# Two heads' weights-times-values matmuls issued one behind the other, each on its half of TensorE's columns

## The chip, the cores and the metric

The kernel runs on one core of a Trainium2 chip. The metric is device time in microseconds (us), the median of several runs. The profiler records one execution of its own. PE is TensorE's matmul stream, PEld its weight loads, DVE VectorE, ACT ScalarE, POOL GpSimd, SP the engine that issues most DMAs.

## What is computed

Two decoder layers over 512 positions of width 1024. Layer 0's mixer joins sliding-window attention (8 query heads, 2 key-value heads of 64 columns) and stick-breaking attention (8 heads of 64). Then follow cross-attention to a memory, a feed-forward part, and layer 1 with another mixer. The part of the reference that matters here, shortened:

```python
def sliding_window_attention(q, k, v, sinks):      # 4 blocks of 128 queries; keys: own block and the one before
    s = jnp.einsum('bnqhgd,bnkhd->bnhgqk', qb, kb) * (HEAD_DIM ** -0.5)
    ...
    p = p / (jnp.sum(p, axis=-1, keepdims=True) + jnp.exp(sink - m))
    o = jnp.einsum('bnhgqk,bnkhd->bnqhgd', p, vb)

def stick_breaking_attention(q, k, v):
    for n in range(S // SB_BLOCK):                  # 4 blocks of 128 queries; keys: all up to the block's end
        z = jnp.einsum('bqhd,bkhd->bhqk', q[:, t0:t1], k[:, :t1]) * (HEAD_DIM ** -0.5)
        ...
        a = jnp.where(causal, jnp.exp(jax.nn.log_sigmoid(z) + log_after), 0.0)
        outs.append(jnp.einsum('bhqk,bkhd->bqhd', a, v[:, :t1]))
```

## The kernel before

All activations are held feature-major (features on partitions, 512 positions along the row). A projection (`proj_fm`, `proj_tm`, lines 176 to 178) is three matmuls per 128-row chunk, since each operand is kept as a high and a low part. The tile framework's scheduler orders each engine's instructions from the program: whatever is ready goes first by priority, so projections of other parts are strewn between the steps of the attention heads. Each engine then runs its list strictly in that order.

Both kinds of heads work in pairs. A pair has one tile `ps_ov` of 128 partitions by 512 positions in PSUM: the first head (`a=0`) writes partitions 0 to 63, the second (`a=1`) 64 to 127. The values have 64 columns, so a weights-times-values matmul has 64 stationary columns and stands on half of the array's columns; the profile shows its form as `128*64`. These operands are plain float32 and each such matmul is run as two passes, each with a weight load of its own; the profile counts passes.

**Window heads**, `swa_pair(i)`, four pairs. Per head: scores (lines 705, 706), softmax, seven transposes (732, 734) into two `ps_tr` tiles, a copy by ACT to `swpT` (736), and seven matmuls over 128 positions (740, 741). `swpT` has one buffer.

**Stick-breaking heads**, `sb_pair(c, ...)`, four pairs. Per head and query block `n`: scores (783, 784) into `ps_at`, two sigmoids (ACT, 786 and 789), triangular masks (POOL), a running product (DVE, 796) and a product (DVE, 798) that leaves the weights in `be0` to `be3`. Then, per key block `kb`, transposes of the blocks `n >= kb` into `ps_tr` (803), a copy by ACT to `sbaT` (805), and one matmul over 512, 384, 256 or 128 positions (806). `ps_tr` and `sbaT` have two buffers each. After the pair, `split` (203 on ACT, 204 on DVE) makes the parts `oh`, `ol` that the output projection reads.

```python
o = ps("ov")
for a in range(2):
    ...
    for kb in range(NT):
        ...
        T.matmul(o[hr, kb * P:], lhsT=vb[h // 4][:, kb, 64 * (h % 4):64 * (h % 4) + 64],
                 rhs=aT[:, kb:].rearrange("p a b -> p (a b)"), start=kb == 0, stop=kb == NT - 1)
```

`mixer0` runs the four window pairs, then the value projections, the four stick-breaking pairs with their projections (`qk_proj`), the output projection of the window heads (`out_proj(0, ...)`), the keys and values of the memory (`mem_prep`, lines 326 to 331, and `mem_kv`), and the output projection of the stick-breaking heads.

Of the kernel before, what the change touches and what calls it, by code (L numbers as in the profile page):

```python
# [18 lines left out]
P = 128  # L19
D = 1024  # L20
KC = D // P
S = 512
NT = S // P
# [10 lines left out]
def trunk(ctx, tc, x, mem, positions, norm_mix, norm_cross, norm_mem, norm_ffn,  # L34
# [30 lines left out]

    def f32(ap):
        return ap.bitcast(FP32)
# [5 lines left out]
    # Token order of the layer 1 mixer: chunks 0 and 2 forwards, then chunks 1 and 3 backwards.  # L73
# [6 lines left out]
    # ------------------------------------------------------------------ constants  # L80
# [67 lines left out]
    # ------------------------------------------------------------------ building blocks  # L148
# [152 lines left out]
    # ------------------------------------------------------------------ memory keys and values  # L301
# [77 lines left out]
    # ------------------------------------------------------------------ cross attention  # L379
# [78 lines left out]
    # ------------------------------------------------------------------ conv feed-forward  # L458
# [44 lines left out]
    # ------------------------------------------------------------------ layer 0 mixer  # L503
    def mixer0():
        W = ab_w_in[0]
        # the tiles of the normalized input hold the memory's parts, keys and values afterwards
# [7 lines left out]
        def rotary():  # L514
            # rotary tables
# [47 lines left out]
        # token-major input blocks and the first weight tile arrive interleaved  # L563
# [28 lines left out]
        # queries as high and low parts stacked by partition halves, keys as both halves' high parts and low parts  # L592
# [10 lines left out]
        # band mask: valid iff i < j <= i + WINDOW  # L603
# [24 lines left out]
        def rope(src, dst, g, nh, tab):  # L628
            cg, sg = tab
            ts = slice(2 * g, 2 * g + 2)  # L630
            V.tensor_tensor(out=dst, in0=src, in1=cg[:, ts].unsqueeze(2).to_broadcast([P, 2, nh, 64]), op=ALU.mult)
            bt = tl(sp, [P, 2 * S], "swpT", 1)[:, :2 * nh * 64].rearrange("p (t h d) -> p t h d", t=2, d=64)
            for s_ in range(2):
                a, b = slice(32 * s_, 32 * s_ + 32), slice(32 * (1 - s_), 32 * (2 - s_))
                V.tensor_tensor(out=bt[:, :, :, a], in0=src[:, :, :, b],
                                in1=sg[:, ts, b].unsqueeze(2).to_broadcast([P, 2, nh, 32]), op=ALU.mult)
            G.tensor_tensor(out=dst, in0=dst, in1=bt, op=ALU.add)

        # inverse norms per token and head
# [50 lines left out]
        def swa_pair(i):  # L690
            o = ps("ov")
            kvs = slice(64 * (i // 2), 64 * (i // 2) + 64)
            for a in range(2):
                h = 2 * i + a
                hr = slice(64 * a, 64 * a + 64)
# [31 lines left out]
                pT = tl(sp, [P, 2 * S], "swpT", 1).rearrange("p (n a q) -> p n a q", n=NT, a=2)  # L727
# [10 lines left out]
                for n in range(NT):  # L738
                    if n:
                        T.matmul(o[hr, n * P:(n + 1) * P], lhsT=va[:, n - 1, kvs], rhs=pT[:, n - 1, 1], start=True, stop=False)  # L740
                    T.matmul(o[hr, n * P:(n + 1) * P], lhsT=va[:, n, kvs], rhs=pT[:, n, 0], start=n == 0, stop=True)  # L741
# [23 lines left out]
        def sb_pair(c, qb, kb_):  # L765
            o = ps("ov")
            for a in range(2):
                hr = slice(64 * a, 64 * a + 64)
                h = 2 * c + a
                # high and low parts of the queries stacked against the high part of the keys twice  # L770
# [7 lines left out]
                at = []  # L778
                for n in range(NT):
                    wdt = (n + 1) * P  # L780
                    z = ps("at")
                    nq = slice(n * P, wdt)
                    T.matmul(z[:, :wdt], lhsT=qs[:, nq], rhs=ks[:, :wdt], start=True, stop=False)
                    T.matmul(z[:, :wdt], lhsT=qs[hr, nq], rhs=kl[hr, :wdt], start=False, stop=True)  # L784
                    be = tl(bp, [P, wdt], f"be{n}", 2)
                    A.activation(out=be[:, :wdt], in_=z[:, :wdt], func=AF.Sigmoid)
                    sn_ = tl(bp, [P, S + 1], "sbs", 2)
                    G.memset(sn_[:, wdt:wdt + 1], 1.0)
                    A.activation(out=sn_[:, :wdt], in_=z[:, :wdt], func=AF.Sigmoid, scale=-1.0)
                    dgs = slice(n * P, wdt)  # L790
                    G.affine_select(out=sn_[:, dgs], in_=sn_[:, dgs], pattern=[[-1, P]], compare_op=ALU.is_gt,
                                    fill=1.0, base=0, channel_multiplier=1)
                    G.affine_select(out=be[:, dgs], in_=be[:, dgs], pattern=[[-1, P]], compare_op=ALU.is_gt,
                                    fill=0.0, base=0, channel_multiplier=1)
                    ex_ = tl(bp, [P, S], "sbe", 2)
                    V.tensor_tensor_scan(out=ex_[:, wdt - 1::-1], data0=sn_[:, wdt:0:-1], data1=sn_[:, wdt:0:-1],
                                         initial=1.0, op0=ALU.mult, op1=ALU.bypass)
                    V.tensor_tensor(out=be[:, :wdt], in0=be[:, :wdt], in1=ex_[:, :wdt], op=ALU.mult)
                    at.append(be)
                for kb in range(NT):  # L800
                    pt = ps("tr", NT, P)
                    for n in range(kb, NT):
                        T.transpose(out=pt[:, n], in_=at[n][:, kb * P:(kb + 1) * P], identity=ident)  # L803
                    aT = tl(bp, [P, NT, P], "sbaT", 2)
                    A.copy(out=aT[:, kb:], in_=pt[:, kb:])
                    T.matmul(o[hr, kb * P:], lhsT=vb[h // 4][:, kb, 64 * (h % 4):64 * (h % 4) + 64],  # L806
                             rhs=aT[:, kb:].rearrange("p a b -> p (a b)"), start=kb == 0, stop=kb == NT - 1)
# [26 lines left out]
        # output projection: window heads first, then the stick-breaking heads  # L834
# [13 lines left out]
    # ------------------------------------------------------------------ layer 1 mixer  # L848
    def mixer1():
# [21 lines left out]
        # Level masks. A level with blocks of h positions pairs neighbouring blocks; sources lie in the earlier one:  # L871
        # the even block of a forward chunk, the odd block of a backward chunk.
        masks = []
        mi = tl(resid, [P, S], "nsq", 2)[:, :P]
        for lv in range(7):
# [3 lines left out]
            for c in range(2):  # L879
                mf = mi[:, c * 64:(c + 1) * 64].rearrange("p (b h) -> p b h", h=h)  # L880
                # 2hb + ch <= s <= 2hb + ch + h - 1
# [19 lines left out]
        def head_core(hd, F, KS, q, vs, e0_, res):  # L901
# [11 lines left out]
            for lv in range(7):  # L913
# [7 lines left out]
                # one stationary tile holds the sources of a forward chunk and, between them, of a backward chunk  # L921
# [81 lines left out]
        def core(pr, args):  # L1003
# [4 lines left out]
            while live:  # L1008
                # the values are projected once both heads' levels are through
                if step == 8:  # L1010
                    vs.append(vproj(pr))
                live = [g for g in live if next(g, g) is not g]
                step += 1
# [45 lines left out]
    # ------------------------------------------------------------------ the two layers  # L1059
# [44 lines left out]
```

## Time and profile before

| | |
|---|---|
| median of 3 runs | 1640.3 us (1640.19 to 1640.34) |
| span of the profiled execution | 1638.4 us |
| PE busy | 1619.5 us, 99% of the span |
| PEld, DVE, ACT, POOL busy | 82%, 62%, 43%, 12% |
| chain that ended last | PE 97%, DVE 1%, DMA 1% |
| granted clock from 80 us on | 1.00 |

The span runs from the first to the last instruction; the 1.9 us between it and the median lie around it. The window heads' matmuls run from 96 to 154 us, the stick-breaking heads' from 184 to 280 us. A row of the timeline gives the start, then the length, of instructions that follow each other with the same line and shape (`x2`: two of them); since matmuls are pipelined, the distance from one start to the next is what a matmul costs the stream, and the length is longer.

### The profile page before, as it was taken

The numbers are of one execution on the slowest core, as the hardware profiler recorded it, in microseconds if no ns is written. First come the engines' busy times: TensorE is split into PE (matmuls) and PEld (weight loads), VectorE is DVE, ScalarE is ACT, GpSimd is POOL, SyncE is SP. The second block draws the span as 40 slices with busy tenths as digits, with TensorE's granted clock in tenths as the row PEclk, the third lists the DMA queues.
The fourth block names the chain that finished last, engine by engine and source line by source line (L and its number), as shares of the span: only waits on it lengthen the run. The fifth ranks groups of instructions, "written<-read, shape, count | busy, mean of one in ns | idle before, by whom it ended". The sixth has DMA issues, their size and how long they took to land.

```text
span 1638.4 us, 21081 instructions
## 1 busy us (share of the span) xinstructions
PE 1619.5 (99%) x8298; PEld 1342.6 (82%) x8298; DVE 1019.0 (62%) x1662; ACT 707.7 (43%) x1246; POOL 201.4 (12%) x307
## 2 busy tenths in 40 slices
PE   7999999999999999999999999999999999999998
PEld 7988677888788888888789898998888788888887
DVE  6764884756576376366776676645556763674563
ACT  5464774555343244133543344543544441342341
POOL 3300341201200000000522133101002000000000
PEclk9999999999999999999999999999999999999999
DMA  6211322411322322322422221443113223223222
GB/s 190 78 42 39 129 78 70 140 52 52 103 93 88 103 89 92 103 82 73 121 66 72 78 78 52 129 155 103 56 48 103 89 92 103 84 96 103 79 82 71
DMA packets 144479, 145.57 MB, mean 89 GB/s; under 512 B 2844, under 2 KB 143837, under 8 KB 144381
## 3 DMA queue, kind: packets, MB, share of 16 engines
q1 hardware_dynamic: 143882, 143.98, 27.5%
q8 instruction: 66, 1.08, 0.3%
q0 software_dynamic: 96, 0.07, 0.1%
q14 instruction: 32, 0.26, 0.1%
q10 hardware_dynamic: 403, 0.18, 0.0%
HBM read 142.12 MB, written 2.10 MB: 88 GB/s over the span
## 4 chain that ended last, share of the span: by engine, by line
PE 97%; DVE 1%; DMA 1%; ACT 0%; issue 0%; SPq 0%; DVEq 0%
PE ps_pj L178 28%; PE ps_pj L176 28%; PE ps_pj L177 28%; PE ps_at L926 1%; PE ps_ov L806 1%; PE ps_tr L803 1%; PE ps_at L784 1%; DMA sbqk<-in_x_dram 1%; PE ps_at L176 1%; PE ps_at L178 1%; PE ps_at L177 0%; PE ps_ov L741 0%; PE ps_ov L958 0%; PE ps_at L906 0%; PE ps_tr L442 0%; PE ps_ov L177 0%
## 5 line engine op out<-in xcount | busy, mean ns | idle before, releaser
L177 PE MATMUL ps_pj<-xl,whi 128*128 128x512 f32 x1088 | 432.2, 397 | 0.0
L178 PE MATMUL ps_pj<-xh,wlo 128*128 128x512 f32 x1024 | 409.2, 400 | 0.0
L176 PE MATMUL ps_pj<-xh,whi 128*128 128x512 f32 x1024 | 403.6, 395 | 2.0 <-DVE hF L977 1.3
L164 ACT CAST whi<-wraw 128x1024 fp32r<-128x1024 f32 (+2 forms) x276 | 263.9, 1004 | 303.9 <-PE ps_pj L177 251.9
L165 DVE TENSOR_TENSOR wlo<-wraw,whi 128x1024 fp32r<-128x1024 f32 (+2 forms) x276 | 318.2, 1188 | 47.3 <-ACT whi L164 46.4
L177 PEld LDWEIGHTS ps_pj<-xl,whi 128*128 128x128 f32 x1088 | 204.4, 188 | 50.1 <-issue 1.0
L176 PEld LDWEIGHTS ps_pj<-xh,whi 128*128 128x128 f32 x1024 | 192.4, 188 | 47.2 <-DVE hF L977 1.9
L178 PEld LDWEIGHTS ps_pj<-xh,wlo 128*128 128x128 f32 x1024 | 192.4, 188 | 44.3 <-issue 1.0
L275 DVE TENSOR_TENSOR xT<-ps_pj,xT 128x512 f32<-128x512 f32 x80 | 53.8, 687 | 153.2 <-PE ps_pj L178 153.0
L177 PE MATMUL ps_pj<-hid,whi 128*128 128x512 f32 x352 | 138.0, 397 | 0.0
L178 PE MATMUL ps_pj<-hid,wlo 128*128 128x512 f32 x352 | 137.8, 397 | 0.0
L176 PE MATMUL ps_pj<-hid,whi 128*128 128x512 f32 x352 | 137.3, 397 | 0.0
L178 PE MATMUL ps_pj<-whi,xl 128*128 128x256 f32 x416 | 120.7, 292 | 1.7 <-DVE xl L226 1.6
L236 POOL TENSOR_TENSOR nacc<-nacc,nsq 128x512 f32<-128x512 f32 x36 | 52.4, 1456 | 523.3 <-ACT nsq L235 520.4
L466 DVE TENSOR_TENSOR fu<-ps_pj,rb 128x512 f32<-128x512 f32 x88 | 60.5, 692 | 90.2 <-PE ps_pj L178 90.1
L177 PE MATMUL ps_pj<-ol,whi 128*128 128x512 f32 x256 | 101.8, 398 | 0.0
L178 PE MATMUL ps_pj<-oh,wlo 128*128 128x512 f32 x256 | 101.5, 398 | 0.0
L176 PE MATMUL ps_pj<-oh,whi 128*128 128x512 f32 x256 | 99.6, 402 | 0.4 <-ACT oh L203 0.4
L468 ACT ACTIVATE fa<-fu,ccol 128x512 f32<-128x512 f32 x88 | 71.3, 814 | 59.3 <-DVE fu L466 59.3
L176 PE MATMUL ps_pj<-whi,xh 128*128 128x256 f32 x288 | 83.4, 291 | 0.0
L177 PE MATMUL ps_pj<-wlo,xh 128*128 128x256 f32 x288 | 82.9, 290 | 0.0
L178 PEld LDWEIGHTS ps_pj<-whi,xl 128*128 128x128 f32 x416 | 79.4, 192 | 3.4 <-DVE xl L226 2.0
(353 smaller groups left out, 2615.6 us busy)
## 6 DMA issues: line engine op xcount, KB each, us to landing
wraw<-in_ffn_w_up_dram SPq DMA_DIRECT2D x44, 1024.0 KB, 5.1
wraw<-in_xa_w_kv_dram SPq DMA_DIRECT2D x16, 1024.0 KB, 5.6
wraw<-in_ffn_w_down_dram SPq DMA_DIRECT2D x16, 1024.0 KB, 5.1
wraw<-in_hgrn_w_in_dram SPq DMA_DIRECT2D x16, 1024.0 KB, 5.6
wraw<-in_ab_w_in_dram SPq DMA_DIRECT2D x8, 1024.0 KB, 5.3
wraw<-in_xa_w_q_dram SPq DMA_DIRECT2D x8, 1024.0 KB, 5.2
wraw<-in_xa_w_o_dram SPq DMA_DIRECT2D x8, 1024.0 KB, 5.3
wraw<-in_ffn_w_down_dram SPq DMA_DIRECT2D x8, 768.0 KB, 4.8
```

What stands on the lines that cost most here:

```text
L164: A.copy(out=hi[:, k, c], in_=raw[:, k, c])
L165: V.tensor_tensor(out=lo[:, k, c], in0=raw[:, k, c], in1=f32(hi[:, k, c]), op=ALU.subtract)
L176: T.matmul(o, lhsT=lh, rhs=rh, start=first, stop=False)
L177: T.matmul(o, lhsT=lh, rhs=rl, start=False, stop=False)
L178: T.matmul(o, lhsT=ll, rhs=rh, start=False, stop=last)
L236: (V if c == KC - 1 else G).tensor_tensor(out=self.acc, in0=self.acc, in1=sq, op=ALU.add)
L275: V.tensor_tensor(out=xT[m], in0=o, in1=xT[m], op=ALU.add)
L466: V.tensor_tensor(out=u, in0=o, in1=rb, op=ALU.mult)
L468: A.activation(out=a, in_=u, func=AF.Identity, scale=conv_col(l, 2, ch), bias=bias_col(l, ch))
L784: T.matmul(z[:, :wdt], lhsT=qs[hr, nq], rhs=kl[hr, :wdt], start=False, stop=True)
L803: T.transpose(out=pt[:, n], in_=at[n][:, kb * P:(kb + 1) * P], identity=ident)
L806: T.matmul(o[hr, kb * P:], lhsT=vb[h // 4][:, kb, 64 * (h % 4):64 * (h % 4) + 64], rhs=aT[:, kb:].rearrange("p a b -> p (a b)"), start=kb ...
```

## The change

In both pairs the transposes and copies of both heads are made first, and then the matmuls of the two heads alternate, the second head's ahead of the first's. The helper `behind` adds an order edge without a semaphore, so that the scheduler keeps the first head's matmul after the second's. In the window pairs `swpT` gets a second buffer; in the stick-breaking pairs `be0` and `be1` get a third, and the matmuls are put under `tc.high_priority()`. The numbers and shapes of instructions stay as they are on every engine; their order changes on PE, ACT, DVE and POOL, and not on SP. Lines after the edits move down by 6 to 27.

```diff
+    def behind(ins, other):
+
+        tc.add_manual_dep(ins.ins if hasattr(ins, "ins") else ins, (other.ins if hasattr(other, "ins") else other).name,
+                          mybir.DependencyInfo(mybir.DependencyClass.NoSync, mybir.DependencyReason.DATA),
+                          reason="side by side")
...
-            bt = tl(sp, [P, 2 * S], "swpT", 1)[:, :2 * nh * 64].rearrange("p (t h d) -> p t h d", t=2, d=64)
+            bt = tl(sp, [P, 2 * S], "swpT", 2)[:, :2 * nh * 64].rearrange("p (t h d) -> p t h d", t=2, d=64)
...
-                pT = tl(sp, [P, 2 * S], "swpT", 1).rearrange("p (n a q) -> p n a q", n=NT, a=2)
+                pT = tl(sp, [P, 2 * S], "swpT", 2).rearrange("p (n a q) -> p n a q", n=NT, a=2)
+                pTs.append(pT)
...
-                for n in range(NT):
-                    if n:
-                        T.matmul(o[hr, n * P:(n + 1) * P], lhsT=va[:, n - 1, kvs], rhs=pT[:, n - 1, 1], start=True, stop=False)
-                    T.matmul(o[hr, n * P:(n + 1) * P], lhsT=va[:, n, kvs], rhs=pT[:, n, 0], start=n == 0, stop=True)
+
+            for n in range(NT):
+                cs_ = slice(n * P, (n + 1) * P)
+                for back in ((1, 0) if n else (0,)):
+                    for a in (1, 0):
+                        mm = T.matmul(o[64 * a:64 * a + 64, cs_], lhsT=va[:, n - back, kvs], rhs=pTs[a][:, n - back, back],
+                                      start=n == 0 or back == 1, stop=back == 0)
+                        if a:
+                            first = mm
+                        else:
+                            behind(mm, first)
...
-                    be = tl(bp, [P, wdt], f"be{n}", 2)
+                    be = tl(bp, [P, wdt], f"be{n}", 3 if n < 2 else 2)
...
-                for kb in range(NT):
+
+            for kb in range(NT):
+                aTs = []
+                for a in range(2):
                     pt = ps("tr", NT, P)
                     for n in range(kb, NT):
-                        T.transpose(out=pt[:, n], in_=at[n][:, kb * P:(kb + 1) * P], identity=ident)
+                        T.transpose(out=pt[:, n], in_=ats[a][n][:, kb * P:(kb + 1) * P], identity=ident)
                     aT = tl(bp, [P, NT, P], "sbaT", 2)
                     A.copy(out=aT[:, kb:], in_=pt[:, kb:])
-                    T.matmul(o[hr, kb * P:], lhsT=vb[h // 4][:, kb, 64 * (h % 4):64 * (h % 4) + 64],
-                             rhs=aT[:, kb:].rearrange("p a b -> p (a b)"), start=kb == 0, stop=kb == NT - 1)
+                    aTs.append(aT)
+
+                with tc.high_priority():
+                    for a in (1, 0):
+                        h = 2 * c + a
+                        mm = T.matmul(o[64 * a:64 * a + 64, kb * P:], lhsT=vb[h // 4][:, kb, 64 * (h % 4):64 * (h % 4) + 64],
+                                      rhs=aTs[a][:, kb:].rearrange("p a b -> p (a b)"), start=kb == 0, stop=kb == NT - 1)
+                        if a:
+                            first = mm
+                        else:
+                            behind(mm, first)
```

On PE, the first window pair before: the seven matmuls of the first head (its weights are `swpT_845`) stand alone, and the transposes of a later head follow.

```order
L177 MATMUL ps_pj_1507<-xl7_229,whi_1474 128x512
L741 MATMUL ps_ov_812<-swpT_845,va_242 64x128
L740 MATMUL ps_ov_812<-swpT_845,va_242 64x128
L741 MATMUL ps_ov_812<-swpT_845,va_242 64x128
L740 MATMUL ps_ov_812<-swpT_845,va_242 64x128
L741 MATMUL ps_ov_812<-swpT_845,va_242 64x128
L740 MATMUL ps_ov_812<-swpT_845,va_242 64x128
L741 MATMUL ps_ov_812<-swpT_845,va_242 64x128
L732 MATMUL ps_tr_897<-ident_70,swp_864 128x128
```

The same pair on PE with the change; `swpT_889` is the second head's, and line 711 is 705 of before.

```order
L711 MATMUL ps_at_1029<-kTh_240,qT0_238 128x128
L750 MATMUL ps_ov_812<-swpT_889,va_242 64x128
L750 MATMUL ps_ov_812<-swpT_845,va_242 64x128
L750 MATMUL ps_ov_812<-swpT_889,va_242 64x128
L750 MATMUL ps_ov_812<-swpT_845,va_242 64x128
L750 MATMUL ps_ov_812<-swpT_889,va_242 64x128
```

The alternation goes on to 14 matmuls; instead of eight groups of seven there are four of 14. The stick-breaking matmuls stood in 24 groups of one or two of the same head, and stand in 16 groups of two, one of each head.

On PE, the end of the last stick-breaking pair before: the second head's first matmuls, with the transposes for its next key blocks between them, and then the first of 30 projection matmuls.

```order
L806 MATMUL ps_ov<-sbaT,vb 64x512
L803 MATMUL ps_tr<-ident,be_2431 128x128
L803 MATMUL ps_tr<-ident,be_2446 128x128
L806 MATMUL ps_ov<-sbaT,vb 64x384
L803 MATMUL ps_tr<-ident,be_2446 128x128
L176 MATMUL ps_pj<-whi,xl_2681 128x256
L177 MATMUL ps_pj<-wlo,xl_2681 128x256
```

The same end with the change; `be_2420` is the second head's block `n=3` and `be_2405` its `n=2`. Lines 821, 829 and 133 are 803, 806 and 127 of before.

```order
L821 MATMUL ps_tr<-ident,be_2420 128x128
L829 MATMUL ps_ov<-sbaT,vb 64x512 x2
L821 MATMUL ps_tr<-ident,be_2390 128x128
L821 MATMUL ps_tr<-ident,be_2405 128x128
L821 MATMUL ps_tr<-ident,be_2420 128x128
L821 MATMUL ps_tr<-ident,be_2337 128x128
L821 MATMUL ps_tr<-ident,be_2352 128x128
L829 MATMUL ps_ov<-sbaT,vb 64x384 x2
L821 MATMUL ps_tr<-ident,be_2405 128x128
L821 MATMUL ps_tr<-ident,be_2420 128x128
L821 MATMUL ps_tr<-ident,be_2352 128x128
L829 MATMUL ps_ov<-sbaT,vb 64x256 x2
```

Behind them stand one transpose, line 133, the two 128-wide matmuls, and three projection matmuls that read this pair's `oh`. No projection matmul is left between these steps. Ahead of the first row stand, from the last score matmul of this pair on (784 of before), four transposes, nine projection matmuls over 512 positions and one more transpose.

## Rows read from the trace of the kernel before

**Rows 1.** The page: busy time by engine, and the chain that ended last.

```profile
PE 1619.5 (99%) x8298; PEld 1342.6 (82%) x8298; DVE 1019.0 (62%) x1662; ACT 707.7 (43%) x1246; POOL 201.4 (12%) x307
PE 97%; DVE 1%; DMA 1%; ACT 0%; issue 0%; SPq 0%; DVEq 0%
```

**Rows 2.** Busy time of each engine in two stretches, with granted clock.

```profile
80.00:160.00 80.00, 80.00 (x461) 66.81 (x460) 45.06 (x153) 44.56 (x114) 0.13 (x2) 1.00 0.13 41
160.00:290.00 130.00, 128.42 (x733) 95.64 (x732) 90.23 (x151) 84.84 (x191) 37.23 (x99) 1.00 0.29 91
```

**Rows 3.** What PE waited for: total us, times, longest.

```profile
PE ps_pj L326 <- DVE xl L331: 1.6, 1, 1.6
```

**Rows 4.** Passes of these matmuls by line, with counts and forms.

```profile
L740 PE MATMUL ps_ov<-swpT,va x48: 272/273/273, 96.1 to 154.0; 128*64 128x128 f32 x48
L741 PE MATMUL ps_ov<-swpT,va x64: 272/273/323, 95.8 to 154.2; 128*64 128x128 f32 x64
L806 PE MATMUL ps_ov<-sbaT,vb x64: 272/458/643, 183.7 to 280.3; 128*64 128x512 f32 x16, 128*64 128x384 f32 x16, 128*64 128x256 f32 x16, 128*64 128x128 f32 x16
```

**Rows 5.** PE's timeline around one window head's group.

```profile
104.04 0.43 PE L741 MATMUL ps_ov<-swpT,va 128*64 128x128 f32 x2
104.31 0.38 PE L740 MATMUL ps_ov<-swpT,va 128*64 128x128 f32 x2
104.53 0.38 PE L741 MATMUL ps_ov<-swpT,va 128*64 128x128 f32 x2
...
105.71 0.33 PE L732 MATMUL ps_tr<-ident,swp 128*128 128x128 f32 x1
105.88 0.27 PE L734 MATMUL ps_tr<-ident,swp 128*128 128x128 f32 x1
105.99 0.27 PE L732 MATMUL ps_tr<-ident,swp 128*128 128x128 f32 x1
```

**Rows 6.** PE's timeline around two stick-breaking matmuls.

```profile
251.22 1.07 PE L806 MATMUL ps_ov<-sbaT,vb 128*64 128x512 f32 x2
252.23 0.44 PE L803 MATMUL ps_tr<-ident,be 128*128 128x128 f32 x2
252.59 0.86 PE L806 MATMUL ps_ov<-sbaT,vb 128*64 128x384 f32 x2
253.38 0.33 PE L803 MATMUL ps_tr<-ident,be 128*128 128x128 f32 x1
```

**Rows 7.** PE's timeline: full weight loads, one column of work each.

```profile
327.20 0.95 PE L411 MATMUL ps_tr<-ones,xsq 128*128 128x1 f32 x8
328.01 0.37 PE L177 MATMUL ps_at<-kl,yh 128*128 128x256 f32 x1
```

**Rows 8.** Timelines of PE, ACT and DVE: one block's way from scores to weights.

```profile
261.47 0.49 PE L784 MATMUL ps_at<-sbkl,sbqs 64*128 64x512 f32 x1
261.89 0.39 PE L177 MATMUL ps_pj<-wlo,xl 128*128 128x256 f32 x1
262.00 0.60 ACT L786 ACTIVATE be<-ps_at 128x512 f32<-128x512 f32 x1 [0.20 <-PE ps_at L784]
264.74 0.69 DVE L798 TENSOR_TENSOR be<-be,sbe 128x512 f32<-128x512 f32 x1
```

**Rows 9.** The copy to sbaT: its lengths (ns), and one behind its transposes.

```profile
L805 ACT COPY sbaT<-ps_tr x32: 267/432/593, 179.4 to 276.3; 128x512 f32<-128x512 f32 x8, 128x384 f32<-128x384 f32 x8, 128x256 f32<-128x256 f32 x8, 128x128 f32<-128x128 f32 x8
274.69 0.44 PE L803 MATMUL ps_tr<-ident,be 128*128 128x128 f32 x2
275.22 0.37 ACT L805 COPY sbaT<-ps_tr 128x256 f32<-128x256 f32 x1 [0.28 <-PE ps_tr L803]
```

**Rows 10.** The last pair's end: its last passes, what follows, the split's cast.

```profile
279.69 0.86 PE L806 MATMUL ps_ov<-sbaT,vb 128*64 128x256 f32 x4
280.49 0.33 PE L127 MATMUL ps_tr<-ident,crow 128*128 128x128 f32 x1
280.60 0.59 ACT L203 CAST oh<-ps_ov 128x512 fp32r<-128x512 f32 x1 [4.06 <-PE ps_ov L806]
```

More of the change, by code (lines that the diff above doesn't have):

```diff
@@ L692, in swa_pair @@
             kvs = slice(64 * (i // 2), 64 * (i // 2) + 64)
+            pTs = []
             for a in range(2):
                 h = 2 * i + a
-                hr = slice(64 * a, 64 * a + 64)
                 pr = tl(sp, [P, NT, 256], "swp", 2)
@@ L766, in sb_pair @@
             o = ps("ov")
+            ats = []
             for a in range(2):
                 hr = slice(64 * a, 64 * a + 64)
-                h = 2 * c + a
                 orow = slice(64 - 64 * a, 128 - 64 * a)
@@ L778, in sb_pair @@
                 at = []
+                ats.append(at)
                 for n in range(NT):
```

## The prediction

> **What bounds the kernel now.** I read the page first, for the engine that is always busy and the chain that ended last: PE is busy 99% of the span, and 97% of the chain is PE [rows 1]. Time that PE saves is therefore time saved, if nothing makes it wait instead. Next the stretches where the changed matmuls stand: from 80 to 160 us, the window heads, PE is never idle; from 160 to 290 us, the stick-breaking heads, it is idle 1.6 us, and the granted clock is 1.00, the 2.4 GHz level, in both [rows 2]. The view of waits puts those 1.6 us down to one wait, in front of the transposes of the memory, for DVE [rows 3]. Then I listed the passes of the lines that the change moves [rows 4], and read PE's timeline around their groups for what one costs [rows 5, 6]. The durations are those of one execution with a span of 1638.4 us; the median of the runs is 1640.3 us, 1.9 us more, and I carry a difference of the span over to it as it is.
>
> **What the matmuls cost.** The window heads have 48 + 64 = 112 passes over 128 positions, the stick-breaking heads 16 of each of four widths [rows 4]. Inside a window group two passes start 0.22 us after the two before them, so a pass is 0.109; the group of 14 takes 105.71 - 104.04 = 1.67 us, and 14 x 0.109 is 1.52, so 0.15 is a fixed cost of the group [rows 5]. With it, the group of two 512-wide passes, 1.01 us, leaves 0.43 for a pass, and that of two 384-wide ones, 0.79 us, leaves 0.32 [rows 6]; cost goes with width, 0.107 per 128 positions, so the 256-wide pass is 0.215 and the four widths together are 1.075. A pass on 64 of the array's 128 columns costs what a full transpose of the same width does (105.88 to 105.99, 0.11 [rows 5]): half of the columns do nothing.
>
> **Fewer groups.** Around a group PE also loses time outside it: the first full transpose behind it takes 0.17 in place of 0.11 [rows 5], and in front, from two transposes to the next group, 0.36 - 0.17 - 0.11 = 0.08 too much [rows 6]. So a group costs 0.15 + 0.06 + 0.08 = 0.29 us in changing from full matmuls to half ones and back. There are 8 + 24 = 32 groups now and 4 + 16 = 20 then: 12 x 0.29 = **3.5 us saved**, whatever the halves do beside each other.
>
> **Side by side.** No row of before has matmuls of both halves next to each other, so I bound this. Nothing is saved if the halves take turns; half of all passes (112 x 0.109 + 16 x 1.075 = 29.4 us) is saved if two heads cost what one does: 14.7 us. I take what follows from starts in program order, as the timelines show them, with the two passes of a matmul one behind the other in their own half: the second pass of one head's matmul then runs beside the first pass of the other's. A window group of 28 passes lasts 15 passes, so 4 x 13 x 0.109 = **5.7 us** saved. A stick-breaking pair of four passes lasts three, since there is nothing to chain on to: 16 pairs save one pass each, 4 x 1.075 = **4.3 us**.
>
> In the window groups two weight loads must fit into each 0.109 us. Eight loads of 128 columns with one column of work each take 328.01 - 327.20 = 0.81 us, 0.10 for one, or 0.115 if the first ran ahead of the group [rows 7]; I take 0.11. One of 64 columns lies between half of that and all of it. I take half, since the first pass of a group, which must wait for its own successor's load, loses no more than some 0.05 of the 0.15 above; the other end is the second rival.
>
> The Trainium skill (TensorE: Matmul & The Clock Gate, Part 3, "Measured speedup vs the span model") reports three column tiles at 2.38 times the speed of one. An estimate from it, two tiles at the same share of the ideal, is 1.59 times, so a window group of 28 x 0.109 = 3.05 us would take 1.92 where I count 1.64, and the 5.7 us would be 4.5. No run here shows it yet.
>
> **New waits.** On PE the order now ends the last stick-breaking pair with no projection between its steps; before, 30 stood there. So each step that ACT makes is bare. A transpose's record ends 0.16 us after the next instruction could start (0.27 long, 0.11 apart [rows 5]); the copy starts 0.09 behind it (274.69 + 0.44 = 275.13, then 275.22 [rows 9]), takes 0.59 for 512 positions to 0.27 for 128 [rows 9], about 0.1 less for each 128; and I allow 0.1 more until PE starts, as long as the way from PE to ACT. Part is spent anyway: 0.1 in entering the group, and the transposes of the next block that stand between (two, one, one). That leaves 0.16 + 0.09 + 0.59 + 0.1 - 0.1 = 0.84 for kb = 0; 0.48 in place of 0.59 and 0.22 off give 0.51 for kb = 1; then 0.38 and 0.11 off, 0.52; then 0.27 and 0.11 off, 0.41. Together 2.3 us.
>
> Ahead of them, the weights of the last block are late. From the start of its score matmul to the end of the product that makes them it is 264.74 + 0.69 - 261.47 = 3.96 us in before [rows 8], with nothing else in its way; with 0.1 until PE starts, 4.06. PE now has behind that matmul its own 0.42 [rows 8], five transposes (0.6) and nine projection matmuls of 512 positions (0.23 each, 2.1): 3.1 us. It stands 0.95 us; 1.6 if DVE, which has a weight split and three products of other blocks in front, is late by as much as that.
>
> Behind them, the first projection that reads this pair needs the cast of `ps_ov`: 0.11 from the last group's end and 0.59 long [rows 10], then 0.1 to PE: 0.8 us. Twelve projection matmuls hid this before. Sum of the tail: 2.3 + 0.95 + 0.8 = **4.0 us lost**, between 2 and 6.
>
> The memory's transposes now stand between the steps of the first pair with hardly a projection near, where DVE has the same running products to make. The wait there was 1.6 us [rows 3]; it can vanish or double, and as the bare stretch is longer I take **1.0 us more**. Elsewhere the order leaves 4 to 39 projection matmuls around each group, and I cost the copies there, the extra buffers and the reordered start at nothing; without that cover a group would lose 0.4 to 0.9 us, as in the tail. What DVE, ACT and POOL do is not less or more than before, and they are busy 62% at most.
>
> **Sum.** 3.5 + 5.7 + 4.3 - 4.0 - 1.0 = 8.5 us. Span 1629.9, median **1631.8 us**, 0.5% less. About 0.2%, 3.3 us, is what a measurement of this kernel can tell from no change. Its own range, with the tail from 2 to 6, the memory's wait from -1.6 to +2.6 and the overlap from 8 to 13 us, is 1627 to 1636. Chance 0.58.
>
> **Rivals.**
>
> *The halves take turns.* Passes of the second half start only when those of the first are through, for instance because their weights can't be loaded while the array streams. Then the 10 us are gone and 3.5 - 5.0 = -1.5 is left: 1641.8, no change that can be told. For it: nothing in this trace shows two halves at work. Against it: in a window group each pass has its own weight load and still starts 0.109 behind the last, so loads do run under streaming there. Chance 0.20. The Trainium skill (TensorE: Matmul & The Clock Gate, Part 3, "The mechanism") says that weight loads overlap with running matmuls only where the row group differs; two column halves have the same rows, and by that rule this rival holds. The window groups' spacing does not agree with it.
>
> *Weight loads bound the window groups.* If a 64-column load takes as long as the 0.11 us of a 128-column one, four passes need 0.44 and nothing is saved there, nor in the 128-wide pairs (4 x 0.109 = 0.44): 3.5 + 3.9 - 5.0 = 2.4 saved, 1637.9. Chance 0.12; within 0.2% in most of these.
>
> *Changing halves costs like changing to half matmuls.* There are 13 such changes in each window group and one in each pair, 4 x 13 + 16 = 68. At 0.15 us, what a group loses inside it [rows 5], that is 10.2 us on top of halves that take turns: 1652, slower. It decides from 0.03 us per change, since the 1.5 us lost there need 1.8 more. Against it: the 0.15 goes with a change between forms, and within a group of one form starts are even. Chance 0.10. The Trainium skill (TensorEngine Tiling, "Key Properties") has a drain for a change of the tiling mode and not for one of the tile; the 0.29 us around each group agrees with the first half, and no row of before shows the second.
>
> **How the numbers follow.** The forecast, 0.58, is faster throughout. Of the second rival, 0.05 is faster and 0.07 within 0.2%; of the first, 0.19 within and 0.01 slower; the third is slower. Faster 0.63, same 0.26, slower 0.11. The range goes from 1627, the forecast's lower end, to 1642.5, past the first two rivals, and leaves out the third and the forecast's far ends, some 0.15.
>
> **What would show it.** Right: PE's busy time down by some 12 to 14 us; window groups of 28 passes that last 1.6 to 1.9 us and stick-breaking pairs 3 passes long, with passes of the second head starting beside the other's; 20 groups; PE idle some 4 us between 250 and 290 us, put down to ACT's copies, one DVE product and the last cast. Wrong: groups as long as the sum of their passes, a gap at each change of halves, or idle time in front of the other pairs, where I count projections as cover.

## The result and the profile after

| | before | changed |
|---|---|---|
| median (4 runs each) | 1640.24 us (1638.2 to 1640.34) | 1627.5 us (1626.29 to 1628.51) |
| ratio | | 0.9929, interval 0.9915 to 0.9943 |
| span of the profiled execution | 1638.4 us | 1626.6 us |

By these medians the change is worth 12.7 us, and 9.3 us where both kernels were run again on another chip (1638.3 and 1629.04, after_again below); 8.5 had been forecast. The direction and the place were right, and the sum was short. (Beside the experiments, on other chips, the kernel before had medians of 1638.3 to 1638.7; the ratio of each kernel below is to the runs of before on its own chip.)

The page after, busy times and chain, beside [rows 1]:

```profile
PE 1604.9 (99%) x8298; PEld 1332.4 (82%) x8298; DVE 1017.4 (63%) x1662; ACT 706.7 (43%) x1246; POOL 200.9 (12%) x307
PE 97%; DVE 1%; ACT 1%; DMA 1%; issue 0%; SPq 0%; POOL 0%; DVEq 0%
```

PE has as many passes as before and is busy 14.6 us less. PE's timeline of one window pair, then the weight loads of the same group, beside [rows 5]:

```profile
99.22 1.75 PE L750 MATMUL ps_ov<-swpT,va 128*64 128x128 f32 x28
100.90 0.33 PE L739 MATMUL ps_tr<-ident,swp 128*128 128x128 f32 x1
101.07 0.27 PE L741 MATMUL ps_tr<-ident,swp 128*128 128x128 f32 x1
```
```profile
99.22 1.51 PEld L750 LDWEIGHTS ps_ov<-swpT,va 128*64 128x64 f32 x28 [0.20 <-ACT ses L723]
```

28 passes last 100.90 - 99.22 = 1.68 us, in each of the four groups, where the 14 of one head lasted 1.67. Their 28 weight loads fit into 1.51 us. Two stick-breaking groups of four passes, beside [rows 6]:

```profile
248.23 1.08 PE L829 MATMUL ps_ov<-sbaT,vb 128*64 128x512 f32 x4
249.24 0.55 PE L821 MATMUL ps_tr<-ident,be 128*128 128x128 f32 x3
...
253.53 0.87 PE L829 MATMUL ps_ov<-sbaT,vb 128*64 128x384 f32 x4
254.33 0.44 PE L821 MATMUL ps_tr<-ident,be 128*128 128x128 f32 x2
```

Four passes last 1.01 and 0.80 us, as two did (1.01 and 0.79). In the trace's records of the 512-wide group, two passes start 7 ns apart, and the other two some 0.48 us later, again 7 ns apart. The records do not name the heads. The two passes of one head alone start one behind the other and fill 1.01 us [rows 6], so I read these as first pass beside first pass, then second beside second.

The two stretches, beside [rows 2], and what PE waited for, beside [rows 3]:

```profile
80.00:160.00 80.00, 80.00 (x480) 65.29 (x479) 48.82 (x153) 48.26 (x126) 2.89 (x10) 1.00 0.17 54
160.00:290.00 130.00, 125.62 (x745) 96.73 (x744) 93.48 (x150) 84.88 (x188) 40.60 (x96) 0.96 0.30 93
```
```profile
PE ps_at L798 <- ACT sbs L804: 1.8, 1, 1.8
PE ps_tr L821 <- DVE be L813: 0.7, 1, 0.7
PE ps_pj L182 <- ACT oh L209: 0.7, 1, 0.7
PE ps_ov L829 <- ACT sbaT L823: 0.7, 1, 0.7
```

Where there was one wait there are four: three of 0.7 us at the end of the last pair, where waits were forecast, and one of 1.8 us in the stretch of the memory's transposes, now in front of a score matmul. The third number from the end of the second window is new too: the granted clock is 0.96 where it was 1.00. PE's timeline around the wait, and the windows behind it:

```profile
175.59 0.38 PE L799 MATMUL ps_at<-sbkl,sbqs 64*128 64x256 f32 x1
177.78 0.62 PE L798 MATMUL ps_at<-sbks,sbqs 128*128 128x384 f32 x1 [1.81 <-ACT sbs L804]
...
182.02 1.97 PE L829 MATMUL ps_ov<-sbaT,vb 128*64 128x512 f32 x4
183.93 0.90 PE L821 MATMUL ps_tr<-ident,be 128*128 128x128 f32 x3
```
```profile
176.00:180.00 4.00, 2.22 (x6) 1.36 (x7) 3.94 (x7) 3.95 (x9) 0.73 (x4) 0.73 0.00 0
180.00:184.00 4.00, 3.86 (x10) 0.97 (x9) 4.00 (x8) 2.75 (x7) 0.88 (x3) 0.50 0.57 170
184.00:188.00 4.00, 4.00 (x19) 4.00 (x20) 2.48 (x5) 2.32 (x5) 0.00 (x0) 0.50 1.04 333
188.00:260.00 72.00, 72.00 (x515) 60.17 (x514) 48.57 (x78) 48.45 (x113) 25.22 (x60) 1.00 0.26 83
```

From 177.9 us on the clock is at 0.50, the 1.2 GHz level, for 10.2 us; the first 512-wide group falls into it and lasts 183.93 - 182.02 = 1.91 us in place of 1.01. PE is busy nearly all of that time, so about half of it, 5.1 us, is lost. Why PE waits is seen in ACT's queue, which has no gap there:

```profile
175.78 0.47 ACT L336 ACTIVATE xl<-ps_pj,gcol 128x256 fp32r<-128x256 f32 x1
176.27 0.62 ACT L790 CAST sbks<-sbks 64x512 fp32r<-64x512 f32 x1
176.92 0.47 ACT L336 ACTIVATE xl<-ps_pj,gcol 128x256 fp32r<-128x256 f32 x1
177.29 0.27 ACT L801 ACTIVATE be<-ps_at 128x128 f32<-128x128 f32 x1
177.45 0.28 ACT L804 ACTIVATE sbs<-ps_at 128x128 f32<-128x128 f32 x1
```

The two sigmoids that free a score buffer stand behind the memory's copies (336) and a cast of keys (790). PE's order has no projection left there: the window heads' projections ran out at 172 us, and those of the memory need these copies.

### The profile page after: what moved, and what is told of

It reads as the page before. It is cut to its first block, busy times and chain, and to the rows that moved or that the text cites. A ratio compares the mean times of both kernels' runs of the same rounds, so it can differ in the third digit from the quotient of the medians.

```text
span 1626.6 us, 21049 instructions
## 1 busy us (share of the span) xinstructions
PE 1604.9 (99%) x8298; PEld 1332.4 (82%) x8298; DVE 1017.4 (63%) x1662; ACT 706.7 (43%) x1246; POOL 200.9 (12%) x307
## 4 chain that ended last, share of the span: by engine, by line
PE 97%; DVE 1%; ACT 1%; DMA 1%; issue 0%; SPq 0%; POOL 0%; DVEq 0%
PE ps_pj L182 28%; PE ps_pj L184 28%; PE ps_pj L183 28%; PE ps_at L953 1%; PE ps_ov L829 1%; PE ps_at L799 1%; DMA sbqk<-in_x_dram 1%; PE ps_tr L821 1%; PE ps_at L182 1%; PE ps_at L184 1%; PE ps_at L183 1%; PE ps_ov L985 0%; PE ps_at L933 0%; PE ps_tr L448 0%; PE ps_ov L750 0%; PE ps_ov L183 0%
## 5 line engine op out<-in xcount | busy, mean ns | idle before, releaser
L475 DVE SCALAR_TENSOR_TENSOR fa<-fu,ccol,fa 128x511 f32<-128x511 f32 x88 | 65.6, 748 | 25.8 <-ACT fa L474 25.8
```

The lines of the kernel that those rows point to most:

```text
L475: V.scalar_tensor_tensor(out=a[:, 1:], in0=u[:, :S - 1], scalar=conv_col(l, 1, ch), in1=a[:, 1:], op0=ALU.mult, op1=ALU.add)
```

## The experiments

Two medians tell little here, since time at the 1.2 GHz level comes and goes between executions: the two traces of the changed kernel (the second is after_again) have 10.2 and 6.8 us of it behind 177 us, and ten of the thirteen traces have 3.4 us of it near 23 us, ahead of the attention heads. So beside the ratio I read from each trace the time from the start of the first window score to the start of PE's last instruction ("stretch"), and for how long the granted clock was at 0.50 in it:

| kernel | median us | ratio to before (interval) | stretch us | at 0.50, us |
|---|---|---|---|---|
| before | 1640.24 | | 1562.1 | 0 |
| changed | 1627.5 | 0.9929 (0.9915 to 0.9943) | 1552.7 | 10.2 |
| after_again | 1629.04 | 0.9941 (0.9926 to 0.9956) | 1551.4 | 6.8 |
| swa_only | 1634.03 | 0.9966 (0.9953 to 0.9979) | 1559.0 | 6.8 |
| sb_only | 1635.97 | 0.9986 (0.9976 to 0.9995) | 1558.5 | 6.8 |
| swa_serial | 1633.31 | 0.9967 (0.9956 to 0.9979) | 1558.2 | 6.8 + 3.4 |
| tail_ring | 1625.84 | 0.9920 (0.9905 to 0.9935) | 1549.3 | 6.8 |
| mem_spread | 1625.18 | 0.9917 (0.9902 to 0.9932) | 1548.2 | 0 |
| spread_ring | 1622.16 | 0.9898 (0.9884 to 0.9913) | 1545.9 | 0 |
| before_spread | 1637.62 | 0.9994 (0.9984 to 1.0003) | 1561.5 | 0 |
| mem_mix | 1624.34 | 0.9913 (0.9898 to 0.9927) | 1548.2 | 0 |
| mix_ring | 1621.84 | 0.9901 (0.9884 to 0.9917) | 1546.0 | 0 |
| warm8 | 1627.22 | 0.9930 (0.9915 to 0.9944) | 1550.8 | 3.4 |

**One kind of heads at a time.** Each kernel takes one of the two pair functions from the kernel before.

Swa_only, with `sb_pair` as before:

```diff
-for kb in range(NT):
-    aTs = []
-    for a in range(2):
+    for kb in range(NT):               # inside "for a in range(2)"
...
-    for a in (1, 0):
-        mm = T.matmul(o[64 * a:64 * a + 64, kb * P:], ...)
+        T.matmul(o[hr, kb * P:], ...)
```

> Only the window heads are paired; the stick-breaking heads stay as in the kernel before. Theory (two halves cost what one does, as the trace after shows): four groups of 1.67 us and four changes of 0.14 us around them are gone, 4 x 1.81 = 7.2 us saved, since PE is never idle in that stretch and no tail is bared: about 1633.0 us beside a kernel before of 1640.2. Rival (the new order of the rest does most of it): less than 4 us saved, 1636 or more. The clock's drop behind 176 us should not be there.

Sb_only, with `swa_pair` as before:

```diff
-for n in range(NT):
-    for back in ((1, 0) if n else (0,)):
-        for a in (1, 0):
-            mm = T.matmul(o[64 * a:64 * a + 64, cs_], ...)
+    for n in range(NT):                # inside "for a in range(2)"
+        if n:
+            T.matmul(o[hr, n * P:(n + 1) * P], lhsT=va[:, n - 1, kvs], ...)
+        T.matmul(o[hr, n * P:(n + 1) * P], lhsT=va[:, n, kvs], ...)
```

> Only the stick-breaking heads are paired; the window heads stay as in the kernel before. Theory: 16 pairs at half the cost (4 x 2.8 / 2 = 5.6 to 8.6 us, by whether a pair's 512-wide passes overlap wholly) and 8 changes of 0.29 us, 10.9 us in all, less some 2.7 us of bare steps at the end of the last pair and some 3 to 5 us of idle time and lower clock behind 176 us: about 1635 us beside 1640.2. If the drop of the granted clock behind 176 us comes from the bare stretch in the first stick-breaking pair, it is here too; rival: if it is missing, the saving is 10 us or more, 1630 or less.

By the medians they save 4.7 and 2.7 us of a median of before of 1638.69, by the ratios 5.6 and 2.3. Each profiled execution has 6.8 us at the lower clock near 181 to 192 us. With half of that added back, the stretches save 3.1 + 3.4 = 6.5 and 3.6 + 3.4 = 7.0 us. The first is near the 7.2 that was expected without a drop; two of its five executions show a granted clock of 1.000 over the whole span, and they take 1630.8 and 1631.4 us, some 6 less than the 1636.8 to 1637.8 of the four of before at that clock. Sb_only had the drop in its expectation, with 1635 us as the number: 5.2 us less than before, of which the medians show about half and the stretch 3.6. So each kind of heads pays, and in each profiled execution the drop takes half of it back. That swa_only has the drop was not expected: its stick-breaking pairs are those of before. But in its timeline no projection stands from 172 to 188 us; in that of before there is none from 182 to 189.5.

**Neighbours in the queue.** Still four groups; within one, first the seven matmuls (14 passes; the text on record calls them 14 matmul instructions) of the second head, then those of the first.

```diff
-for n in range(NT):
-    for back in ((1, 0) if n else (0,)):
-        for a in (1, 0):
+for a in (1, 0):
+    for n in range(NT):
+        for back in ((1, 0) if n else (0,)):
```

> The changed kernel, with the 14 matmul instructions of one head of a window pair issued ahead of the 14 of the other instead of in turns, still four groups. Theory (it is the neighbouring of the two halves that pays): a window group takes 28 x 0.109 + 0.15 = 3.2 us in place of 1.68, so 4 x 1.5 = 6.1 us are given back, 1633.6 where the changed kernel has 1627.5. Rival (halves overlap wherever they stand in the queue, or it is the smaller number of groups that pays): within 1.5 us of the changed kernel.

PE's timeline of its first group:

```profile
100.17 2.89 PE L750 MATMUL ps_ov<-swpT,va 128*64 128x128 f32 x28
102.99 0.33 PE L739 MATMUL ps_tr<-ident,swp 128*128 128x128 f32 x1
```

2.82 us in place of 1.68, in all four groups: 4 x 1.14 = 4.6 us are given back, and the stretch, with as long at the lower clock as the changed kernel, is 5.5 us longer; the other 0.9 is idle time that PE has more of between 160 and 200 us (2.86 and 1.95). The theory holds for the window groups, and the rival falls; the stick-breaking pairs had no such run. That it is 2.82 and not the 3.2 of all passes in a row has a cause in the records: at the change of heads, the first passes of the half that comes second in the order start between the last ones of the other. Of its time at 0.50, 3.4 us stand behind the end of the last pair, from 281.7 us on; the changed kernel, with the same waits there, has none in either trace.

**The end of the last pair.** Its second and fourth key block take other buffers.

```diff
-pt = ps("tr", NT, P)
+pt = ps("at" if c == 3 and kb % 2 else "tr", NT, P)
...
-aT = tl(bp, [P, NT, P], "sbaT", 2)
+if c == 3 and kb % 2:
+    aT = tl(bp, [P, S], "sbe", 2).rearrange("p (a b) -> p a b", b=P)
+else:
+    aT = tl(bp, [P, NT, P], "sbaT", 2)
```

> The changed kernel, but the last stick-breaking pair puts its second and fourth key block's transposes into the score buffers and their copies into the scan buffers, which are idle by then, so that they need not wait for the block before. Forecast of the prediction (each copy is bared, 2.3 us in all): 1.0 to 1.5 us less than the changed kernel. Rival (only the first copy, the last block's weights and the last cast are bared, which this edit leaves): within 0.6 us of the changed kernel, the waits of 0.7 us for the weights, the first copy and the cast unchanged.

PE's timeline at the end of the last pair, the changed kernel first, then tail_ring:

```profile
264.73 0.40 PE L798 MATMUL ps_at<-sbks,sbqs 128*128 128x512 f32 x1
...
269.07 0.33 PE L821 MATMUL ps_tr<-ident,be 128*128 128x128 f32 x1 [0.72 <-DVE be L813]
270.07 1.08 PE L829 MATMUL ps_ov<-sbaT,vb 128*64 128x512 f32 x4 [0.68 <-ACT sbaT L823]
271.08 1.07 PE L821 MATMUL ps_tr<-ident,be 128*128 128x128 f32 x5
272.20 0.87 PE L829 MATMUL ps_ov<-sbaT,vb 128*64 128x384 f32 x4
273.00 0.85 PE L821 MATMUL ps_tr<-ident,be 128*128 128x128 f32 x3
273.89 0.65 PE L829 MATMUL ps_ov<-sbaT,vb 128*64 128x256 f32 x4
...
276.28 0.96 PE L182 MATMUL ps_pj<-oh,whi 128*128 128x512 f32 x3 [0.68 <-ACT oh L209]
```
```profile
264.77 0.40 PE L798 MATMUL ps_at<-sbks,sbqs 128*128 128x512 f32 x1
...
269.12 0.33 PE L821 MATMUL ps_tr<-ident,be 128*128 128x128 f32 x1 [0.19 <-DVE be L813]
269.29 0.27 PE L821 MATMUL ps_at<-ident,be 128*128 128x128 f32 x1
270.12 1.08 PE L832 MATMUL ps_ov<-sbaT,vb 128*64 128x512 f32 x4 [0.57 <-ACT sbaT L826]
271.13 0.44 PE L821 MATMUL ps_tr<-ident,be 128*128 128x128 f32 x2
271.50 0.87 PE L832 MATMUL ps_ov<-sbe,vb 128*64 128x384 f32 x4
272.30 0.33 PE L821 MATMUL ps_at<-ident,be 128*128 128x128 f32 x1
...
274.22 0.96 PE L182 MATMUL ps_pj<-oh,whi 128*128 128x512 f32 x3 [0.69 <-ACT oh L209]
```

From the last block's scores to the first projection that reads the pair it is 276.28 - 264.73 = 11.55 us in the changed kernel and 9.45 in tail_ring: 2.1 us less, more than the 1.0 to 1.5 expected. All of it lies behind the first group, which starts 5.34 and 5.35 us behind the scores. The later copies were bared as well, with only transposes beside them, and the rival falls. But not all of the 2.1 us were waits for them: six transposes, 0.65 us, now stand ahead of the first group, three of them in the wait for the last block's weights, which is 0.19 us in place of 0.72.

**The memory's transposes, spread out.** The memory gets tiles of its own and another DMA queue, so that its load no longer waits for the weights' buffers, and its four transpose blocks are issued among the window heads' projections.

```diff
-raw = tl(wp, [P, MT, D], "wraw", 2)
-SY.dma_start(out=raw, in_=mem_tm)
+rs = [rtile(i) for i in range(2 * MT)]
+for i in range(2 * MT):
+    G.dma_start(out=rs[i], in_=mem_tm[:, i // 2, (i % 2) * 512:(i % 2 + 1) * 512])
...
-for mm in range(4):
-    out_proj(0, mm)
+prep, block = mem_prep(0, ...)
+out_proj(0, 0)
+out_proj(0, 1)
+out_proj(0, 2)
+block(0)
+block(1)
+out_proj(0, 3)
+block(2)
+block(3)
```

Mem_spread. 

> The changed kernel, with the memory loaded into tiles of its own and its four transpose blocks put among the last window-head projections instead of behind them, so that 12 projections stand between the first two blocks and the third, and 14 behind the fourth. The last pair's order is as in the changed kernel. Theory (the bare stretch in the first stick-breaking pair costs twice: 1.8 us of idle time, and then 7 to 10 us at the 1.2 GHz level, worth half of that): no wait above 1 us and no granted clock below 1.00 between 160 and 200 us, 5 to 7 us less than the changed kernel, about 1621.5. Rival (the clock falls there whatever stands around the pair, or the idle time was slack): the drop is still in the trace and the time is within 2 us of the changed kernel.

Spread_ring, with the edit of tail_ring as well. 

> The kernel with the spread memory transposes and the last pair's own buffers together. If the two losses are separate, their gains add: 1.7 to 2.1 us less than with the spread alone, about 1619.5. Rival (both sit on the same chain, so that what one gives back the other waits for): no more than 0.5 us less than the better of the two alone.

Before_spread, the same move in the kernel before. 

> The kernel before with the same move of the memory's transposes. Theory: it has only the one wait of 1.6 us there and no drop of the clock, so at most 1.6 us less, 1637 beside 1638.7. Rival (the move is worth as much to any kernel): 5 us less, 1634.

Mem_mix, with `block(mm)` behind each `out_proj(0, mm)`. 

> The changed kernel with one memory block behind each of the four window-head projections. Around 176 us it has still more cover, but in its order the memory's projections run out earlier: from the second key block of the third pair to the end of the last pair only 9 projections are left. Theory (a bare stretch costs idle time and then the clock, wherever it stands): no drop near 176 us, and idle time and a drop of the clock between 250 and 280 us in its place, so no more than 3 us less than the changed kernel. Rival (only the memory's copies make the loss): as fast as the kernel with the spread transposes.

The windows from 176 us on, mem_spread:

```profile
176.00:180.00 4.00, 4.00 (x27) 3.19 (x26) 3.94 (x7) 3.95 (x10) 1.73 (x6) 1.00 0.00 0
180.00:184.00 4.00, 3.00 (x19) 1.87 (x17) 4.00 (x7) 2.74 (x6) 1.45 (x2) 1.00 0.02 6
```

The drop is gone, and the stretch is 4.5 us shorter than that of the changed kernel, where the drop was worth 5.1; the 0.6 between them is not accounted for. The idle time is not gone: it is now 1.0 us there, in front of a projection (the second row has 3.00 of 4.00 us busy), and smaller waits elsewhere (PE is idle for 1.73 us from 160 to 200 us, 1.95 in the changed kernel). So it was the clock that cost, and the 5 to 7 us expected counted the wait as well, wrongly. The medians show less, 1625.2 for 1627.5.

The other executions have no trace, but each has a granted clock for its whole span, to three digits. Its mean is 0.9966 over the eight of the changed kernel, 0.9984 over the 16 of the four kernels that have this move on top of it, and 0.9989 over the 37 of before on the experiments' chips. One minus the clock, times the span, is the time lost to it: 5.5, 2.5 and 1.9 us on average. So neither the loss nor its going is confined to the traced executions, but the average loss by the change, 3.6 us, is smaller than the 5.1 of the trace. Where in the span the time was lost these numbers do not tell. The move changes the memory's load as well as the order, and no run parts the two.

In the kernel before the move is worth 0.6 us in the stretch and nothing that can be told in the median, in line with what was expected: the traced execution has no drop there to lose. Of the 1.6 us that PE waited there, nothing is left in before_spread, so a wait can be worth less than its length. In spread_ring the two gains add: 2.3 us more in the stretch, 3.0 in the median.

Mem_mix went the rival's way. Its end is barer, and yet the clock stays at 1.00 there, with waits of 0.8, 0.7 and 0.7 us in the last pair; its stretch is that of mem_spread to 0.1 us. "A bare stretch wherever it stands" is too wide a theory for this execution; that of swa_serial, whose last pair has waits of 0.7, 0.7 and 0.7 us, did lose the clock behind them.

**Filling the idle time.** Eight matmuls that nobody reads, in front of the score matmul that waits.

```diff
+if c == 0:
+    for _ in range(8):
+        warm.append(T.matmul(o[:, :P], lhsT=ident, rhs=ident, start=True, stop=True))
...
+if c == 1 and a == 0 and n == 1:
+    for d in warm:
+        behind(d, zz)      # zz: the block's second score matmul
```

After_again. 

> The changed kernel once more, beside the others on one chip: 1626 to 1628.5 us, and a drop of the granted clock of 7 to 10 us from about 178 us on in the trace, if it belongs to the kernel and not to one execution.

Warm8. 

> The changed kernel, with eight matmuls of the identity by itself (their result is overwritten and used by nobody) put in PE's order exactly where it is idle for 1.8 us in the second pair's third block: 8 matmuls of two passes of 0.107 us are 1.7 us. Theory A (the idle time makes the clock fall): the idle time is filled, the clock stays at 1.00, and the time is 3 to 5 us less than the changed kernel although more work is done: 1623 to 1624.5. Theory B (the bare stretch as a whole, with its short matmuls, or something else than idle time, makes it fall): the drop stays, and the time is within 1 us of the changed kernel.

Mix_ring. 

> The kernel with one memory block behind each window-head projection, and the last pair's own buffers. The two gains add as they did with the other spread: some 2 to 3 us less than the mixed memory blocks alone, about 1622. Rival: its bare stretch is longer (from the second key block of the third pair on), so the last pair's waits come from other steps than the buffers, and the ring is worth less than 1 us.

PE's timeline in warm8, then a window from 160 to 200 us of the changed kernel, and of warm8:

```profile
176.82 2.05 PE L823 MATMUL ps_ov<-ident 128*128 128x128 f32 x16
178.70 0.44 PE L800 MATMUL ps_at<-sbks,sbqs 128*128 128x384 f32 x1
...
181.51 0.51 PE L800 MATMUL ps_at<-sbks,sbqs 128*128 128x512 f32 x1 [0.61 <-ACT sbs L809]
```
```profile
160.00:200.00 40.00, 38.05 (x194) 27.98 (x193) 31.34 (x54) 28.84 (x66) 13.07 (x36) 0.87 0.33 106
```
```profile
160.00:200.00 40.00, 38.97 (x217) 29.09 (x216) 32.74 (x57) 29.63 (x69) 13.08 (x39) 0.96 0.32 106
```

The drop is in the second traced execution of the changed kernel as well (6.8 us from 178.2 us on), so it belongs to the kernel; the median, 1629.04, is 0.5 us above what was expected. In warm8 the wait is filled and the score matmul is as fast as ever, 0.44 us in place of 0.62, but the drop comes all the same, later (from 182.5 us, behind the 0.61 us of idle time) and shorter, 3.4 us. By the medians the kernel with work that is good for nothing is 1.8 us faster (1627.22 and 1629.04 on one chip, with intervals that overlap, so not clear of noise), by the stretch 0.6 and 1.9. Neither theory holds as put: the idle time is not all that makes the drop. That it has a part in it is not shown, since the two traces of the changed kernel differ by 3.4 us of drop themselves. In mix_ring the end's buffers are worth 2.2 us in the stretch on top of the mixed blocks, and 2.5 between the medians (of two chips); the rival falls.

Both spread_ring and mix_ring beat the changed kernel, at a ratio of 0.990 to the kernel before against 0.993 and 0.994; mix_ring and after_again ran on one chip, and their intervals do not overlap.

## Why the prediction fell short

1. **Fewer groups, 3.5 us.** 20 groups came, and entering and leaving one costs what it did: 0.15 us inside (1.68 is 14 x 0.109 and 0.15), and 0.17 in place of 0.11 for the first transpose behind it (100.90 to 101.07). It had no run of its own.
2. **Side by side, 10.0 us: the step that failed, in size.** "I take what follows from starts in program order, [...] with the two passes of a matmul one behind the other in their own half." The passes do not wait for each other in that order: first pass beside first pass, second beside second. A window group lasts 1.68 us where 15 x 0.109 + 0.15 = 1.79 was forecast, and a 512-wide pair 1.01 where three passes would be 1.44. What was put down as the bound, 14.7 us, is what it is, outside the 8 to 13 us that the range allowed; for the window groups swa_serial shows that it is the order in the queue that pays it.
3. **The tail, 4.0 us.** Waits of 0.72 (0.95 forecast) for the last block's weights and 0.68 (0.8) for the cast. The copies had 2.3. The view of waits shows only one of PE's waits for them, 0.68 us, but the starts in the timeline above show more: from the transpose at 269.07 us to the projection at 276.28 it is 7.2 us, and the work between takes some 4.5 by the spacings read elsewhere (eleven transposes 1.4, four groups 2.8, entering them 0.3). That leaves 2.7 us, some 2.1 of them for the copies. Together 3.5. Tail_ring gets 2.1 us back.
4. **The memory, 1.0 us more.** The wait is 1.8 us where it was 1.6, 0.2 more and well inside the bounds; it stands at another instruction and is for ACT, not DVE.
5. **The clock, not in the sum.** I took the granted clock of 1.00 in both stretches [rows 2] for a constant. In the traced execution the bared stretch of the memory cost 10.2 us at the 1.2 GHz level, 5.1 us, more than any wait; over all executions the change costs 3.6 us by the clock.

So the sum with measured terms is 3.5 + 14.7 - 3.5 - 0.2 - 5.1 = 9.4 us, and the stretch is 9.5 us shorter. The other 2.3 us between the two spans lie ahead of the first window score (71.7 and 69.4 us): the execution of before has 3.4 us at 0.50 at 23.5 us, which that of the changed kernel has not, and which can be 1.7 of them; that part is chance and not the change. The span is 3.3 us under the forecast 1629.9: 4.7 by point 2, 0.5 and 0.8 by points 3 and 4, and 2.3 by the start are 8.3, and the clock takes 5.1 of them back. Two errors of some 5 us, one in each direction, hid behind a forecast that came out near: that the time fell into the range was in part luck.

The rivals fall with the first rows. Halves that take turns would have made a window group 3.2 us long. By the rule of the Trainium skill named there (TensorE: Matmul & The Clock Gate, Part 3, "The mechanism"), that a weight load overlaps only with a running matmul of another row group, they should have; the two halves have the same rows, and 28 loads run under 28 passes in 1.51 us, so the measurement decides against it as it stands. (The same section of the Trainium skill also lets a load into the background weight buffer go ahead; no run here shows which buffer these loads used.) The same rows answer the second rival: two loads of 64 columns fit into each 0.109 us. And 13 changes of half in a group cost nothing that shows (1.68 for 1.67), which is the third. The estimate from the Trainium skill (TensorE: Matmul & The Clock Gate, Part 3, "Measured speedup vs the span model"), from three tiles at 2.38 times the speed of one, was 1.59 for two; measured without the fixed 0.15 us it is 3.05 / 1.53 = 2.0.

## What to carry to other kernels

Two matmuls that each fill half of the array's columns should be neighbours in PE's order, half by half; then two cost what one does (1.68 us for 1.67 in a window group), at 64 stationary columns, in plain float32, and with weight loads of their own. To make them neighbours the work around them moves, and the price is there: count which stretch loses its last independent matmul, and read the granted clock as well as the waits in it, in more than one execution. The view of waits showed 1.8 us there; the windows with the granted clock showed the 10 us behind it.

## What was not expected of the hardware

- Passes of the two halves run out of the order of the queue: of two neighbouring matmuls, the later one's first pass starts 7 ns behind the earlier one's first, ahead of the earlier one's second pass; and in swa_serial a half whose matmuls stand behind seven others starts before these are through, 0.4 us early.
- The granted clock fell to 0.50 behind a wait of 1.8 us (changed kernel in both traces, swa_serial, tail_ring), of 1.7 us (sb_only), of 1.4 us (swa_only), and once behind the last pair's waits of 0.7 us (swa_serial). It did not fall behind one of 1.6 us [rows 3] (before) nor of 1.0 us (mem_spread), and in warm8 it fell with no wait longer than 0.61 us ahead of it. What in the stretch decides it stays open. That spreading the memory's transposes takes the drop near 180 us away was seen in the one profiled execution of each of the four kernels that have that move on top of the changed one, and their 16 executions lose 2.5 us each by the clock on average, where those of the changed kernel lose 5.5.
